# A transposed copy of the input for the first layer, and high and low weights side by side in a 136-column block

## The chip, the cores and the metric

The kernel runs on one core of a Trainium2 chip. The metric is the device time of one execution in microseconds (us). A core has five engines that run their own instruction streams in order: TensorE (PE: matmuls and transposes, results into PSUM), VectorE (DVE), ScalarE (ACT), GpSimd (POOL) and SyncE (SP). SyncE issues most of the DMAs here, ScalarE a few (`nc.scalar`).

## The reference, cut to what matters

Two layers of a gated mixer with 256 rows of 2048 channels. Each normalizes its input, multiplies it with a wide input matrix, runs four branches on slices of the product, and merges them by gates:

```python
def _layer(x, positions, norm_g, w_in, ..., w_up, merge_b, w_out):
    h = _rmsnorm(x, norm_g)
    proj = h @ w_in
    (a_q, a_k, a_v, a_z, b_cq, b_ckv, b_kr, b_z, c_qk, c_v, c_i, c_f, c_o, c_z,
     d_u, d_z, gate) = jnp.split(proj, idx, axis=-1)
    ya = _branch_dilated(a_q, a_k, a_v, a_qn_g, a_kn_g) * jax.nn.silu(a_z)
    yb = _branch_mla(...) * jax.nn.silu(b_z)
    yc = _branch_mlstm(...) * jax.nn.silu(c_z)
    yd = _branch_s5(...) * jax.nn.silu(d_z)
    up = jnp.einsum('bsnw,nwd->bsnd', jnp.stack([ya, yb, yc, yd], axis=2), w_up)
    gates = jax.nn.sigmoid((gate + merge_b).astype(jnp.float32)).reshape(Bsz, S, N_BRANCH, D_MODEL)
    merged = jnp.sum(gates * up.astype(jnp.float32), axis=2).astype(x.dtype)
    return x + merged @ w_out
```

`_rmsnorm` divides each row by the root of its mean square and scales it by `norm_g`. Branch d (`_branch_s5`) holds a linear recurrence along the rows.

## The kernel before

**Products in two parts.** Every weight tile `raw` (float32, by DMA) is split into a high part `wh` (a cast on ScalarE to the reduced format fp32r) and a low part `wl = raw − wh` (VectorE). The normalized input is split likewise into `hH` and `hL`. A product of one slice of 128 input channels (index k) and one half of the rows (t = 0, 1) is three matmuls into the same PSUM tile: `hH·wh`, `hH·wl`, `hL·wh`.

**Blocks and units.** A block is one slice of output columns over all k: 512 columns nearly everywhere, 136 in block `x`, which holds `b_ckv` (128 columns) and the gates `c_i`, `c_f` (8). The weights of a block come in units: 2 k of 512 columns, or 4 k of 136 (`_units`, L96). In layer 0 units 0 to 7 are block `cqkr`, 8 to 15 `du`, 16 to 19 `x`, 20 to 27 `cqk`; then come the other branch inputs (`aq1`, `ak1`, ... for branch a) with gate blocks (`g01`, ...) and their up-projections between them. A unit of 512 columns is 12 matmuls. `Stream` keeps three units split ahead and six loaded ahead; `raw`, `wh` and `wl` have four buffers each, so the load, the cast and the difference of a unit wait until the unit four before has been used.

**PSUM.** Large blocks take two of four banks `mm`, so the next block but one waits until the results have been read: by `aqk` (VectorE, blocks `aq` and `ak`), `gate` (VectorE, gate blocks), `bj`, `kr` and `blat` (ScalarE, blocks `cqkr` and `x`) and others.

**The order of the side work.** The program text is recorded once. All branch work is written as generators in chains; after each unit `tick` runs steps of them. `Plan` keeps an estimated clock for every engine and the estimated time at which every tile is ready, and `tick` takes a step when its inputs are ready by that estimate and no other engine's clock is too far ahead of TensorE's. The order of instructions on each engine thus follows from the estimates; on the chip the order is fixed and every engine follows it. Steps that matter below: `dm` (the scan of branch d along the rows), `dk` and `dr` (eight short steps that reduce an angle for branch d, VectorE), `rsi`, `rsy`, `rst`, `ass` (an inverse root by Newton steps, the first two on VectorE, the others on POOL), on which `aqk` depends.

**The start.** `win` unit 0 and the input come first on SyncE's queue (L1353 and following). The input tiles `xb` have the rows on the partitions; `prep_h` transposes them on TensorE (`xt`, 8 transposes of 128x128 for each of four chunks of 512 channels), and ScalarE and VectorE make `hH` and `hL` of the result. `squares` sums the squares of `xb` on ScalarE (`sq`, with a read of the accumulator after each); after the last one `finish_norm` reduces them (`r`, VectorE) and takes the inverse root on POOL. The norm factor `r` is applied when a block's result is read, so block `cqkr` can run before `r` is known, but `bj`, its first reader on ScalarE, waits for it. Eight matmuls on zeros (`warm`, L1352) stand at the very start.

All instructions of the engines are recorded through a helper, so the trace shows them with its line (L253 before), and all loads with L272.

Of the kernel before, what the change touches and what calls it, by code (L numbers as in the profile page):

```python
# [8 lines left out]
F32 = mybir.dt.float32  # L9
# [6 lines left out]
P = 128  # L16
S = 256
# [75 lines left out]
NCOL = {nm: len(c) for nm, c in COLS}  # L93


def _units(K, n):  # L96
    u = max(1, min(K, 1024 // n))
    while K % u:
        u -= 1
    return [(k0, u) for k0 in range(0, K, u)]  # L100
# [155 lines left out]


@with_exitstack
def hybrid_kernel(ctx: ExitStack, tc: tile.TileContext, x_in, pos, win, wup, wout, wuq, wukv, wglu, pp_in, db_in,
                  dc_in, glub_in, mb_in, cc_in, id_in, out, depth=2, dbg=None):  # L260
    nc = tc.nc
    plan = Plan(nc)
# [92 lines left out]
    class Stream:  # L355
# [5 lines left out]
        def dma(self, upto):  # L361
            while self.nd <= min(upto, len(units) - 1):
                _, dram, off, kk, n = units[self.nd]
                t = wp.tile([P, kk * n], F32, tag="raw", name="raw", bufs=4)
                load(nc.sync, t, in_=dram[off:off + P * kk * n].rearrange("(p f) -> p f", p=P))
                self.raw[self.nd] = t
                self.nd += 1

        def split(self, upto):
            while self.ns <= min(upto, len(units) - 1):  # L370
                self.dma(self.ns)
                i = self.ns
                _, _, _, kk, n = units[i]
                raw = self.raw.pop(i)
                wh = wp.tile([P, kk, n], F32R, tag="wh", name="wh", bufs=4)
                wl = wp.tile([P, kk, n], F32R, tag="wl", name="wl", bufs=4)
                rv = raw.rearrange("p (k n) -> p k n", n=n)
                if i >= 4:
                    for a, b in zip((wh, wl), self.names.pop(i - 4)):
                        plan.used[a.name] = plan.used[b]  # L380
                self.names[i] = (wh.name, wl.name)
                A.copy(wh, rv)
                V.tensor_tensor(wl, rv, wh, op=ALU.subtract)
                self.spl[i] = (wh, wl)
                self.ns += 1

        def get(self, i):
# [40 lines left out]
    def until(name, ready):  # L428
        while not ready() and step(name):
            pass  # L430

    def block(key, lhs, K, n):

        small = key[1] in ("uq", "ukv", "glu")
        ps = [brps(f"mb{t}") if small else mmps(f"mm{t}") for t in range(2)]
        if small:
            plan.pins.update(p.name for p in ps)
        k = 0
        while k < K:
            assert units[cur[0]][0] == key, (units[cur[0]][0], key)  # L440
            lhs(k, 0)
            wh, wl = stream.get(cur[0])
            if cur[0]:
                lhs(min(k + 4, K - 1), 0)
            kk = units[cur[0]][3]
            cur[0] += 1
            for j in range(kk):
                for t in range(2):
                    hH, hL = lhs(k, t)
                    o = ps[t][:, :n]  # L450
                    T.matmul(o, lhsT=hH, rhs=wh[:, j, :], start=(k == 0), stop=False)
                    T.matmul(o, lhsT=hH, rhs=wl[:, j, :], start=False, stop=False)
                    T.matmul(o, lhsT=hL, rhs=wh[:, j, :], start=False, stop=(k == K - 1))
                k += 1
            tick()
        if not small:
            drain("e")
        return ps
# [115 lines left out]
    def prep_h(o, d, xb):  # L574
# [17 lines left out]
                                       op0=ALU.mult, op1=ALU.subtract)  # L592
        o.hH[d], o.hL[d] = hH, hL

    def squares(o, d, xb):
        yield (xb,)
        for t in range(2):
# [15 lines left out]

    def lhs_of(H, Lo, chain="m"):
        def lhs(k, t):
            until(chain, lambda: Lo[k // 4] is not None)
            return H[k // 4][:, k % 4, t * P:(t + 1) * P], Lo[k // 4][:, k % 4, t * P:(t + 1) * P]

        return lhs
# [730 lines left out]
    ps = brps("warm")  # L1350
    for i in range(WARM):
        nc.tensor.matmul(ps, lhsT=zero[:, 0:P], rhs=zero, start=True, stop=True)  # L1352
    stream.dma(0)  # L1353
    for d in range(4):
        xb = s4([P, 2, 512], name="xb")
        if d == 0:
            for i in range(2):
                q = slice(256 * i, 256 * i + 256)
                load(nc.sync, xb[:, :, q], in_=x_cur[0][:, :, q])
        else:  # L1360
            load(nc.sync, xb, in_=x_cur[d])
        spawn("m", prep_h(o, d, xb))
        spawn("q", squares(o, d, xb))
        stream.dma(min(2 * d + 1, 3))
    load(nc.sync, cc, in_=cc_in)
    stream.split(0)
    step("m")
    spawn("q", rotary_tables())

    for l in range(depth):  # L1370
# [35 lines left out]
        for kind, nm in layer_sequence(l):  # L1406
            if kind == "in":
# [13 lines left out]
                    b_kr(o, ps)  # L1421
                    spawn("e", b_latent(o, ps, 448, 512, "cqg", "cqT"))
                elif nm == "x":
                    c_if(o, ps)
                    spawn("e", b_latent(o, ps, 128, 128, "ckvg", "ckT"))
                elif nm == "cqk":
                    o.cqk = copy_r(o, ps, 512, "cqk")
                    spawn("c", c_conv(o))
# [96 lines left out]
def _layout(inp):  # L1525
# [65 lines left out]
    for i, n in enumerate(("d_c_re", "d_c_im")):  # L1591
        a = f[n].reshape(dep, 16, 2, 16, 64).transpose(0, 2, 4, 1, 3)
        for g in range(2):
# [1 line left out]
    glu = f["d_glu_w"].reshape(dep, 2, 2, P, 512).transpose(0, 1, 3, 2, 4).reshape(dep, -1)  # L1595
    x = f["x"].reshape(2, P, D).transpose(1, 0, 2)
    pos = f["positions"].reshape(2, P).T
    arrs = dict(x_in=x, pos=pos, win=win, wup=wup, wout=wout, wuq=wuq, wukv=wukv, pp_in=pp,
                db_in=db.reshape(dep, P, 512), dc_in=dc.reshape(dep, P, 1024), wglu=glu, glub_in=f["d_glu_b"],
                mb_in=f["merge_b"], cc_in=_consts(), id_in=np.eye(P, dtype=np.float32))  # L1600
    return {k: np.ascontiguousarray(v) for k, v in arrs.items()}
# [18 lines left out]
```

## Time and profile before

| | us |
|---|---|
| median of 3 runs (lowest, highest) | 2090.07 (2087.39, 2090.59) |
| profiled execution | 2088.86 |
| its span in the trace | 2086.7 |
| TensorE busy | 2065.0 |
| VectorE busy | 1418.9 |
| ScalarE busy | 1034.8 |
| GpSimd busy | 446.9 |
| TensorE waiting for VectorE's `aqk`, `gate`, `wl` | 7.9, 3.9, 2.6 |

The span is that of one profiled execution on the chip. Busy time of TensorE counts matmuls whose ends are modelled, so it is an upper bound of its work; how long a matmul really occupies it is seen in the distance between the starts of two.

### The profile page before, as it was taken

The page shows a single profiled execution, that of the slowest core. Times are in us where ns is not written, and L with a number is a line of the kernel's source. Part 1 is how long each engine was busy: PE and PEld are TensorE (multiplying, and loading weights), DVE is VectorE, ACT ScalarE, POOL GpSimd, SP SyncE. Part 2 cuts the span into 40 slices and gives each one's busy share as a digit, 9 for nine tenths or more (in the row PEclk, how much of TensorE's full clock was granted, in tenths as well). Part 3 has the DMA queues.
Part 4 walks back from the last instruction along what each step waited for, and adds up shares of the span by engine and source line. Part 5 has one row for each costly group of instructions (what it writes and reads, how often), then busy time and mean ns, then how long its engine had stood idle before and what let it go on. Part 6 is the DMA issues. An engine that isn't in the chain of part 4 may idle for free.

```text
span 2086.7 us, 26821 instructions
## 1 busy us (share of the span) xinstructions
PE 2065.0 (99%) x9764; PEld 1702.1 (82%) x9764; DVE 1418.9 (68%) x1817; ACT 1034.8 (50%) x1574; POOL 446.9 (21%) x702
## 2 busy tenths in 40 slices
PE   9999999999999999999999999999999999999999
PEld 7888887788888888888888888887777888888887
DVE  5566578778777766667556765858777667667664
ACT  6656464454544544444456564455554445444442
POOL 2533114321242000001043121323223300001010
PEclk9999999999999999999999999999999999999999
DMA  7554354445555556656655543455445555556564
GB/s 266 182 187 166 123 176 167 156 163 170 183 191 173 183 199 206 204 202 208 232 188 182 192 162 124 175 166 191 163 167 187 185 178 183 205 204 205 197 212 171
DMA packets 111012, 384.60 MB, mean 184 GB/s; under 512 B 12321, under 2 KB 13217, under 8 KB 110881
## 3 DMA queue, kind: packets, MB, share of 16 engines
q1 hardware_dynamic: 108576, 378.40, 53.2%
q10 hardware_dynamic: 2304, 4.50, 0.6%
q8 instruction: 76, 1.25, 0.2%
q14 instruction: 56, 0.45, 0.1%
HBM read 378.66 MB, written 4.19 MB: 183 GB/s over the span
## 4 chain that ended last, share of the span: by engine, by line
PE 95%; DVE 3%; DMA 1%; POOL 1%; ACT 0%; issue 0%; SPq 0%; DVEq 0%; ACTq 0%
PE mm L253 86%; PE mb L253 2%; PE pv L253 1%; DVE dk L253 1%; PE tt L253 1%; PE dyp L253 1%; PE sc L253 1%; PE dbu L253 1%; DVE wl L253 1%; DVE dm L253 1%; DVE dr L253 1%; PE bsc L253 1%; PE pt L253 1%; DMA raw<-win 0%; PE xt L253 0%
## 5 line engine op out<-in xcount | busy, mean ns | idle before, releaser
L253 DVE TENSOR_TENSOR wl<-raw,wh 128x1024 fp32r<-128x1024 f32 (+1 forms) x694 | 909.0, 1323 | 533.8 <-ACT wh L253 530.8
L253 ACT CAST wh<-raw 128x1024 fp32r<-128x1024 f32 (+1 forms) x694 | 722.8, 1046 | 805.2 <-PE mm L253 690.7
L253 PE MATMUL mm<-wh,hH 128*128 128x512 f32 (+1 forms) x2240 | 877.0, 392 | 6.3 <-DVE gate L253 3.9
L253 PE MATMUL mm<-wl,hH 128*128 128x512 f32 (+1 forms) x2240 | 867.5, 387 | 2.6 <-DVE wl L253 2.6
L253 PE MATMUL mm<-wh,hL 128*128 128x512 f32 (+1 forms) x2240 | 866.7, 387 | 0.0
L253 PEld LDWEIGHTS mm<-wh,hH 128*128 128x128 f32 x2240 | 421.6, 188 | 97.5 <-issue 10.8
L253 PEld LDWEIGHTS mm<-wl,hH 128*128 128x128 f32 x2240 | 422.1, 188 | 88.0 <-DVE wl L253 5.5
L253 PEld LDWEIGHTS mm<-wh,hL 128*128 128x128 f32 x2240 | 421.6, 188 | 86.5 <-DVE hL L253 0.4
L253 POOL TENSOR_TENSOR gate<-gate 128x1024 f32<-128x1024 f32 x24 | 62.5, 2603 | 590.9 <-DVE gate L253 590.9
L253 POOL TENSOR_TENSOR dm<-dm,dm 128x256 f32<-128x256 f32 x64 | 76.3, 1213 | 354.9 <-DVE dm L253 345.9
L253 PE MATMUL mm<-wh,yH 128*128 128x512 f32 x256 | 101.3, 396 | 5.5 <-DVE aqk L253 5.5
L253 PE MATMUL mm<-wl,yH 128*128 128x512 f32 x256 | 100.6, 393 | 0.0
L253 PE MATMUL mm<-wh,yL 128*128 128x512 f32 x256 | 100.4, 392 | 0.0
L253 PE MATMUL mm<-wh,mH 128*128 128x512 f32 x256 | 100.2, 391 | 0.0
L253 PE MATMUL mm<-wh,mL 128*128 128x512 f32 x256 | 99.6, 389 | 0.0
L253 PE MATMUL mm<-wl,mH 128*128 128x512 f32 x256 | 99.6, 389 | 0.0
L253 POOL TENSOR_TENSOR dm<-dm,cosT 128x512 f32<-128x512 f32 x32 | 48.9, 1529 | 85.0 <-DVE dm L253 84.9
L253 PEld LDWEIGHTS mm<-wh,yH 128*128 128x128 f32 x256 | 48.7, 190 | 16.0 <-issue 5.9
L253 PEld LDWEIGHTS mm<-wh,yL 128*128 128x128 f32 x256 | 48.6, 190 | 10.2
L253 PEld LDWEIGHTS mm<-wl,yH 128*128 128x128 f32 x256 | 48.7, 190 | 9.8
L253 PEld LDWEIGHTS mm<-wh,mL 128*128 128x128 f32 x256 | 48.0, 188 | 9.9
L253 PEld LDWEIGHTS mm<-wh,mH 128*128 128x128 f32 x256 | 48.1, 188 | 9.8
(351 smaller groups left out, 1704.2 us busy)
## 6 DMA issues: line engine op xcount, KB each, us to landing
raw<-win SPq DMA_DIRECT2D x544, 512.0 KB, 3.7
raw<-wup SPq DMA_DIRECT2D x64, 512.0 KB, 4.2
raw<-wout SPq DMA_DIRECT2D x64, 512.0 KB, 4.2
mb<-mb_in SPq DMA_DIRECT2D x32, 256.0 KB, 4.4
xb<-x_in SPq DMA_DIRECT2D x7, 512.0 KB, 6.6
raw<-wuq SPq DMA_DIRECT2D x6, 512.0 KB, 4.1
raw<-win SPq DMA_DIRECT2D x8, 272.0 KB, 2.8
raw<-wglu SPq DMA_DIRECT2D x4, 512.0 KB, 4.4
```

What stands on the lines that cost most here:

```text
L253: return fn(*args, **kw)
```

## The change

The host lays out a second copy of the input, `xt_in`, with channels on the partitions (`x` reshaped and transposed). In layer 0, `prep_first` makes `hH` and `hL` from it, k by k, without TensorE and PSUM. The first load is chunk 0's slice k = 0, then unit 0 in two halves, then k = 1 to 3, all on SyncE; the other three chunks are issued by ScalarE. The untransposed `xb` are still needed for the squares: `first_squares` loads them on ScalarE's queue, the third and fourth each after the squares of an earlier one, and the constants `cc` after them. So the input is read twice.

In block `x`, a unit is 2 k instead of 4, `wh` and `wl` share one tile, and a (k, t) step is two matmuls: `hH` with `[wh | wl]`, 272 columns, and `hL` with `wh`, 136. The second half of the result is copied out of PSUM (`xlo`, ScalarE) and added to the first (VectorE); the readers of the block then take the sum from SBUF. This holds in both layers.

```diff
+NX = 136
 def _units(K, n):
-    u = max(1, min(K, 1024 // n))
+    u = max(1, min(K, 1024 // (2 * n if n == NX else n)))
...
-                load(nc.sync, t, in_=dram[off:off + P * kk * n].rearrange("(p f) -> p f", p=P))
+                src = dram[off:off + P * kk * n].rearrange("(p f) -> p f", p=P)
+                for q in (slice(0, n), slice(n, kk * n)) if self.nd == 0 else (slice(0, kk * n),):
+                    load(nc.sync, t[:, q], in_=src[:, q])
...
+                if n == NX:
+                    both = wp.tile([P, kk, 2, n], F32R, tag="wh", name="wh", bufs=4)
+                    wh, wl = both[:, :, 0], both[:, :, 1]
...
-                A.copy(wh, rv)
-                V.tensor_tensor(wl, rv, wh, op=ALU.subtract)
-                self.spl[i] = (wh, wl)
+                for q in (slice(0, 1), slice(1, kk)) if i == 0 else (slice(0, kk),):
+                    A.copy(wh[:, q], rv[:, q])
+                    V.tensor_tensor(wl[:, q], rv[:, q], wh[:, q], op=ALU.subtract)
+                self.spl[i] = (wh, both if n == NX else wl)
...
+                    if n == NX:
+                        two = [(ps[t][:, :2 * n], hH, wl[:, j].rearrange("p a n -> p (a n)")), (o, hL, wh[:, j])]
+                        for a, h, w in two if k < K - 1 else two[::-1]:
+                            T.matmul(a, lhsT=h, rhs=w, start=(k == 0 and h is hH), stop=(k == K - 1 and h is hH))
+                        continue
...
+    def prep_first(o, d, xt):
+        hH, hL = s4([P, 4, S], F32R, name="hH"), s4([P, 4, S], F32R, name="hL")
+        o.hH[d], o.hL[d] = hH, hL
+        for k2 in (0, 2):
+            yield (xt,)
+            for k in (k2, k2 + 1):
+                g = o.p("norm_g")[:, 4 * d + k:4 * d + k + 1]
+                A.activation(hH[:, k], xt[:, k], AF.Copy, scale=g)
+                V.scalar_tensor_tensor(hL[:, k], xt[:, k], g, hH[:, k].bitcast(F32), op0=ALU.mult, op1=ALU.subtract)
+            o.nh = 4 * d + k2 + 2
+
+    def first_squares(o):
+        xb = {}
+        yield
+        for d in range(5):
+            if d < 4:
+                xb[d] = s4([P, 2, 512], name="xb")
+                load(nc.scalar, xb[d], in_=x_cur[d])
+            else:
+                load(nc.sync, cc, in_=cc_in)
+            if d:
+                yield from squares(o, d - 1, xb[d - 1])
...
-    stream.dma(0)
+    first, o.nh = o, 0
     for d in range(4):
-        xb = s4([P, 2, 512], name="xb")
+        xt = s4([P, 4, S], name="xt")
         if d == 0:
-            for i in range(2):
-                q = slice(256 * i, 256 * i + 256)
-                load(nc.sync, xb[:, :, q], in_=x_cur[0][:, :, q])
+            load(nc.sync, xt[:, 0:1], in_=xt_in[:, 0:1])
+            stream.dma(0)
+            load(nc.sync, xt[:, 1:4], in_=xt_in[:, 1:4])
         else:
-            load(nc.sync, xb, in_=x_cur[d])
-        spawn("m", prep_h(o, d, xb))
-        spawn("q", squares(o, d, xb))
-        stream.dma(min(2 * d + 1, 3))
-    load(nc.sync, cc, in_=cc_in)
-    stream.split(0)
-    step("m")
+            load(nc.scalar, xt, in_=xt_in[:, 4 * d:4 * d + 4])
+        spawn("m", prep_first(o, d, xt))
+        if d == 0:
+            stream.dma(3)
+            step("m")
+            step("m")
+            stream.split(0)
+    spawn("q", first_squares(o))
...
-                    c_if(o, ps)
-                    spawn("e", b_latent(o, ps, 128, 128, "ckvg", "ckT"))
+                    lo = parp.tile([P, 2, NX], F32, tag="xlo", name="xlo", bufs=1)
+                    xs = [lo[:, t] for t in range(2)]
+                    for t in range(2):
+                        A.copy(xs[t], ps[t][:, NX:2 * NX])
+                    for t in range(2):
+                        V.tensor_tensor(xs[t], ps[t][:, :NX], xs[t], op=ALU.add)
+                    c_if(o, xs)
+                    spawn("e", b_latent(o, xs, 128, 128, "ckvg", "ckT"))
```

Since the estimates change, the planner also deals out layer 0's side work in another order. Three places follow. First ScalarE in block `cqkr` of layer 0, from the casts of units 5 to 7 to the first reader of the norm factor, before:

```order
L253 CAST wh<-raw 128x1024 x3
L253 ACTIVATE hH<-xt,pp 128x256 x4
L253 CAST wh<-raw 128x1024
L253 ACTIVATE sq,ss<-xb 128x512
L253 ACTIVATE dt<-pp 128x16
L253 CAST wh<-raw 128x1024
L253 ACTIVATE mag<-mag 128x16
L253 CAST wh<-raw 128x1024
L253 ACTIVATE bj,bss<-mm_132,r 128x64
```

and after, from the casts of units 6 to 8:

```order
L256 CAST wh<-raw 128x1024 x3
L256 ACTIVATE hH<-xt,pp 128x256 x2
L256 CAST wh<-raw 128x1024
L256 ACTIVATE sq,ss<-xb 128x512 x4
L256 ACTIVATE dt<-pp 128x16
L256 CAST wh<-raw 128x1024
L256 ACTIVATE mag<-mag 128x16
L256 ACTIVATE bj,bss<-mm_140,r 128x64
```

In both, ten units (1 to 10) and the first one have been cast when `bj` comes; four squares instead of one stand behind the cast of unit 9 (unit 8 before).

Second, VectorE in block `av1` of layer 0, around the reading of block `ak1` (`aqk`), before:

```order
L253 TENSOR_SCALAR rsi<-ass 128x8
L253 TENSOR_SCALAR rsy<-rsi 128x8
L253 TENSOR_TENSOR wl<-raw,wh 128x1024 x2
L253 SCALAR_TENSOR_TENSOR dm_3666<-mag,dm_3665 128x256 x2
L253 SCALAR_TENSOR_TENSOR dk<-cc,dhi,dk 128x256
L253 SCALAR_TENSOR_TENSOR dr<-cc,dlo,dk 128x256
...
L253 TENSOR_TENSOR wl<-raw,wh 128x1024
L253 TENSOR_TENSOR aqk<-mm_3496,ass 128x512
L253 TENSOR_TENSOR aqk<-mm_3497,ass 128x512
```

and after:

```order
L256 TENSOR_SCALAR rsi<-ass 128x8
L256 TENSOR_SCALAR rsy<-rsi 128x8
L256 TENSOR_TENSOR wl<-raw,wh 128x1024 x2
L256 TENSOR_TENSOR aqk<-mm_3441,ass 128x512
L256 TENSOR_TENSOR aqk<-mm_3442,ass 128x512
L256 TENSOR_TENSOR wl<-raw,wh 128x1024
L256 SCALAR_TENSOR_TENSOR dr<-cosT,dk 128x1024
```

The scan (`dm`, two steps) and the four pairs of `dk` and `dr` no longer stand between `rsy` and `aqk`; they now stand one block of branch a earlier, behind the reading of `aq1`, with two `gate` steps after them.

Third, TensorE in block `x`, one k, before:

```order
L253 MATMUL mm_642<-wh,hH 128x136
L253 MATMUL mm_642<-wl,hH 128x136
L253 MATMUL mm_642<-wh,hL 128x136
L253 MATMUL mm_643<-wh,hH 128x136
L253 MATMUL mm_643<-wl,hH 128x136
L253 MATMUL mm_643<-wh,hL 128x136
```

and two k after:

```order
L256 MATMUL mm_610<-wh,hH 128x272
L256 MATMUL mm_610<-wh,hL 128x136
L256 MATMUL mm_611<-wh,hH 128x272
L256 MATMUL mm_611<-wh,hL 128x136
L256 MATMUL mm_610<-wh,hH 128x272
L256 MATMUL mm_610<-wh,hL 128x136
```

Two matmuls take the place of three for each k and t.

## Rows read from the trace of the kernel before

**Rows 1.** Page, part 1: busy us of each engine, share, instructions

```profile
PE 2065.0 (99%) x9764; PEld 1702.1 (82%) x9764; DVE 1418.9 (68%) x1817; ACT 1034.8 (50%) x1574; POOL 446.9 (21%) x702
```

**Rows 2.** Waits of TensorE: us in total, times, longest

```profile
PE mm L253 <- DVE aqk L253: 7.9, 2, 5.5
PE mm L253 <- DVE gate L253: 3.9, 1, 3.9
PE mm L253 <- DVE wl L253: 2.6, 4, 1.6
```

**Rows 3.** Windows, layer 0: us; busy (count) PE, PEld, DVE, ACT, POOL; PEclk; DMA; GB/s

```profile
346.00:350.00 4.00, 2.68 (x12) 2.22 (x13) 4.00 (x5) 3.38 (x17) 0.54 (x1) 1.00 0.40 139
...
365.00:370.00 5.00, 5.00 (x17) 3.98 (x16) 2.73 (x3) 1.05 (x1) 1.55 (x2) 0.69 0.29 105
...
415.00:420.00 5.00, 2.25 (x5) 1.84 (x6) 4.96 (x8) 0.00 (x0) 0.00 (x0) 0.59 0.28 105
420.00:425.00 5.00, 5.00 (x18) 4.01 (x17) 1.48 (x2) 1.89 (x2) 0.00 (x0) 0.73 0.31 107
```

**Rows 4.** Timeline, TensorE, block `x`, layer 0 (96 of 136 columns): start, us, instruction

```profile
55.27 0.22 PE L253 MATMUL mm<-wh,hH 128*128 128x136 f32 x1
...
65.94 0.45 PE L253 MATMUL mm<-wh,hH 128*128 128x512 f32 x1
```

**Rows 5.** Chain that ended last: start, us, matmuls; `mb` has 256 columns, `mm` 512

```profile
118.20 2.87 PE mb L253 x24
121.08 9.09 PE mm L253 x40
```

**Rows 6.** Timelines, ScalarE and VectorE, and DMA landing: feeding one unit

```profile
58.10 1.05 ACT L253 CAST wh<-raw 128x1024 fp32r<-128x1024 f32 x1 [1.41 <-PE mm L253]
...
59.18 1.23 DVE L253 TENSOR_TENSOR wl<-raw,wh 128x1024 fp32r<-128x1024 f32 x1 [1.57 <-ACT wh L253]
...
raw<-win SPq DMA_DIRECT2D x8, 512.0 KB, 3.2
```

**Rows 7.** Timelines, VectorE and TensorE, at the two `aqk` waits

```profile
360.54 1.27 DVE L253 TENSOR_TENSOR_SCAN dm<-mag,dm 128x256 f32<-128x256 f32 x2
362.49 1.29 DVE L253 TENSOR_TENSOR aqk<-mm,ass 128x512 f32<-128x512 f32 x2 [0.68 <-POOL ass L253]
...
409.05 1.27 DVE L253 TENSOR_TENSOR_SCAN dm<-mag,dm 128x256 f32<-128x256 f32 x2
...
415.79 1.22 DVE L253 TENSOR_TENSOR wl<-raw,wh 128x1024 fp32r<-128x1024 f32 x1
416.93 1.28 DVE L253 TENSOR_TENSOR aqk<-mm,ass 128x512 f32<-128x512 f32 x2
...
417.75 0.77 PE L253 MATMUL mm<-wh,yH 128*128 128x512 f32 x1 [5.53 <-DVE aqk L253]
```

**Rows 8.** The start: chain, DMA landing at 8 to 12 us, window

```profile
8.32 3.52 PE mm L253 x12
11.85 0.87 PE xt L253 x8
12.72 2.77 PE mm L253 x12
...
raw<-win SPq DMA_DIRECT2D x2, 512.0 KB, 9.1
...
10.00:12.00 2.00, 2.00 (x12) 1.62 (x11) 1.33 (x2) 2.00 (x8) 0.00 (x0) 1.00 1.01 401
```

**Rows 9.** Timelines, ScalarE, VectorE and POOL: from the last square to `bj`

```profile
26.51 0.62 ACT L253 ACTIVATE sq<-xb 128x512 f32<-128x512 f32 x1
...
30.50 0.15 DVE L253 TENSOR_REDUCE r<-ss 128x2 f32<-128x8 f32 x1
...
37.52 0.20 POOL L253 TENSOR_TENSOR r<-rst,rsy 128x2 f32<-128x2 f32 x1
37.75 0.32 ACT L253 ACTIVATE bj<-mm,r 128x64 f32<-128x64 f32 x1 [5.71 <-POOL r L253]
```

More of the change, by code (lines that the diff above doesn't have):

```diff
@@ L258, in hybrid_kernel @@
 @with_exitstack
-def hybrid_kernel(ctx: ExitStack, tc: tile.TileContext, x_in, pos, win, wup, wout, wuq, wukv, wglu, pp_in, db_in,
+def hybrid_kernel(ctx: ExitStack, tc: tile.TileContext, x_in, xt_in, pos, win, wup, wout, wuq, wukv, wglu, pp_in, db_in,
                   dc_in, glub_in, mb_in, cc_in, id_in, out, depth=2, dbg=None):
@@ L374, in split @@
                 raw = self.raw.pop(i)
-                wh = wp.tile([P, kk, n], F32R, tag="wh", name="wh", bufs=4)
-                wl = wp.tile([P, kk, n], F32R, tag="wl", name="wl", bufs=4)
+                if n == NX:
+                    both = wp.tile([P, kk, 2, n], F32R, tag="wh", name="wh", bufs=4)
+                    wh, wl = both[:, :, 0], both[:, :, 1]
+                else:
+                    wh = wp.tile([P, kk, n], F32R, tag="wh", name="wh", bufs=4)
+                    wl = wp.tile([P, kk, n], F32R, tag="wl", name="wl", bufs=4)
                 rv = raw.rearrange("p (k n) -> p k n", n=n)
@@ L593, in prep_h @@
         o.hH[d], o.hL[d] = hH, hL
+    def prep_first(o, d, xt):
[15 more added lines that the diff above has]
+                load(nc.scalar, xb[d], in_=x_cur[d])
+            else:
+                load(nc.sync, cc, in_=cc_in)
+            if d:
+                yield from squares(o, d - 1, xb[d - 1])
     def squares(o, d, xb):
@@ L615, in lhs @@
         def lhs(k, t):
-            until(chain, lambda: Lo[k // 4] is not None)
+            until(chain, lambda: Lo[k // 4] is not None and (chain != "m" or Lo is not first.hL or first.nh > k))
             return H[k // 4][:, k % 4, t * P:(t + 1) * P], Lo[k // 4][:, k % 4, t * P:(t + 1) * P]
@@ L1597, in _layout @@
     pos = f["positions"].reshape(2, P).T
-    arrs = dict(x_in=x, pos=pos, win=win, wup=wup, wout=wout, wuq=wuq, wukv=wukv, pp_in=pp,
+    xt = f["x"].reshape(S, 16, P).transpose(2, 1, 0)
+    arrs = dict(x_in=x, xt_in=xt, pos=pos, win=win, wup=wup, wout=wout, wuq=wuq, wukv=wukv, pp_in=pp,
                 db_in=db.reshape(dep, P, 512), dc_in=dc.reshape(dep, P, 1024), wglu=glu, glub_in=f["d_glu_b"],
```

## The prediction

> **What bounds the kernel now.** I read the busy shares first: TensorE works 99% of the span, VectorE 68%, ScalarE 50% [rows 1]. So a saving counts only where TensorE issues less, waits less or runs at a higher granted clock. The waits of TensorE come next: two waits for `aqk` hold 7.9 us, one for `gate` 3.9, four for `wl` 2.6 [rows 2]. Then the stretches around the waits of layer 0: at 346 us TensorE is busy only 2.68 of 4 us, and after the two `aqk` waits the granted clock is 0.69, 0.59 and 0.73 in the five-microsecond windows, between the 1.2 and the 2.4 GHz level [rows 3]. The price of a matmul comes from the x block and from the chain [rows 4, 5], the price of feeding one from ScalarE and VectorE [rows 6], the two `aqk` waits from the timelines [rows 7], and the start from the chain, a DMA row and the rows that lead to `r` [rows 8, 9]. The profiled execution took 2088.86 us, 1.2 under the median 2090.07; I sum against the former and add 1.2 at the end. 4.2 us (0.2%) is about what a measurement of this kernel can tell from no change.
>
> **The x block.** Its 96 matmuls of 136 columns run from 55.27 to 65.94 us, 10.67 us, 111 ns each [rows 4]. A 512-column matmul is 9.09/40 = 227 ns, a 256-column one 2.87/24 = 119.6 ns [rows 5]. So 136 columns sit on a floor that does not shrink with the columns. A matmul of 272 columns appears nowhere; on the line through 256 and 512 columns it is 119.6 + 16 × 107.4/256 = 126 ns. Its bounds are 119.6 (no dearer than 256) and 227. The middle of these is no better guess than the line, since 272 lies next to 256, so I take 126. A (k, t) step then costs 126 + 111 = 237 instead of 333 ns: 96 ns less, 32 steps a layer, two layers: −6.1 us. The added work is small: two copies, two adds and eight more weight-tile DMAs, on engines that have room; the x block's result is read a block later and nobody on TensorE waits for it soon. What shrinks is the cover. The block gets shorter, 7.6 instead of 10.7 us, and is cut into units of two k. The first unit of the next block needs a raw buffer that the fifth x unit gives back at about block start + 2.1; its load lands 3.2 later, cast 1.05 and difference 1.23 follow [rows 6], which is start + 7.6 with the gaps between them, where TensorE wants it at + 7.6. I charge 0.7 us for both layers (0 to 2.6, the upper end if each layer waits for a whole 1.23 us difference). **Net −5.4** (−6.1 to −3.5).
>
> The Trainium skill, page "TensorE: Matmul & The Clock Gate", section "Back-to-back issue gap", gives an isolated gap of N/2.4 + 2.5 ns, that is 59 ns for 136 and 116 for 272 columns; by that the fusion would save 2.5 ns a pair, 0.2 us in all. The row of 111 ns [rows 4] speaks against it here; a saving near zero is a rival below all the same.
>
> **The order of layer 0.** The edits change the planner's clocks, so layer 0's side work is dealt out anew, layer 1's not. Two waits lie there. The first: block `aq1`'s evacuation `aqk` starts at 362.49, behind a scan and a POOL result, while TensorE stands [rows 7]. The second: a scan starts at 409.05, eight `dk`/`dr` steps follow, `wl` at 415.79, and `aqk` only at 416.93; TensorE resumes at 417.75 after 5.53 us [rows 7]. In the changed order both `aqk` pairs come ahead of the scan and the eight steps: the first has its POOL chain started two units (5.4 us) earlier and comes one `wl` earlier, the second has no burst ahead of it. Cost now: `wl` 1.6 us near 347 [rows 2, 3]; 7.9 us of `aqk`; and the clock: 17 matmuls where 22 fit in 365 to 370 us (−1.1), 5 × 227 ns of work in 2.25 busy us (−1.1) and 18 for 22 (−0.9) after the second [rows 3]. Sum 1.6 + 7.9 + 3.1 = 12.6. What is late next: the burst now stands after the first `aqk` with two `gate` steps behind it. By the rows it occupies 415.79 − 409.05 = 6.7 us, and two `gate` steps about as long as two `aqk`, 1.3 [rows 7], then `wl` 1.23: 9.3 us from one `wl` to the next. Usually these lie 2.72 us apart (twelve matmuls at 227 ns) and each is done 8.2 − 2.3 = 5.9 us before TensorE needs it, since its buffer comes free three units ahead [rows 6]. 9.3 − 2.7 − 5.9 = 0.7 us of wait. A later `aqk` (block `aq2`) stands two units lower than before, behind the `wl` that is done 2.3 us after the last unit ahead of the block that wants its banks has begun; that unit lasts 2.7, the two steps 1.3, so 0.3 to 0.9 of wait: 0.7. **Gain 12.6 − 1.4, −11** (−12.6 to −5, the latter if one wait of the second's size, 5.5 + 2.0, comes back). The `gate` wait of 3.9 us is in layer 1 and stays [rows 2].
>
> **The start, first twelve units.** Three groups of eight transposes leave TensorE, 0.87 us each [rows 8]: −2.6. The first matmul needs 1 MB landed, as before, but no transposes between: I put it at 7.6 instead of 8.3, −0.7. The first twelve matmuls cost 3.52 us against 2.77 later, with the transposes just ahead of them [rows 8]; with nothing ahead of them since the warm-up I double that loss: +0.8 (0 to 1.5). ScalarE now multiplies every chunk from `xt`, and its squares wait for `xb`, which is loaded on ScalarE's own queue behind three `xt` chunks. In order behind those squares stand the casts of units 2, 5 and 6. Loads ran at 401 GB/s here and a weight tile took 9.1 us to land [rows 8], so 2 MB more in the same stretch is 5 us of transfers. I charge 2.4 us of waits (0 to 4). These four terms cancel: unit 11 would start at about 41.7 us, as before.
>
> The Trainium skill, "DMA: Bandwidth & Descriptors", section "Issuing engines are not separate DMA queues", says that loads started by different engines interleave on the same 16 DMA engines; by it the charge tends to its upper end, 1.6 us more. No run here shows two large streams from two queues.
>
> **The start, the norm.** ScalarE's `bj` waits for `r`: the last square at 26.51 us, the reduction at 30.50, `r` done at 37.72, `bj` at 37.75 after 5.71 us idle [rows 9]. Behind `bj` stands the cast of unit 11. Before, one more square was left at that point; now four are, and all behind the cast of unit 9, whose buffer TensorE frees at 41.7 − 5 × 2.72 = 28.1. Cast 1.05: 29.2; four squares with their accumulator reads, 0.8 each: 32.4; cast of unit 10 and two small steps: 33.7; its `wl`, 34.9, stands ahead of the reduction; then the same 7.2 us: `r` at 42.2. `bj` and `kr` 1.0, cast 1.05, `wl` 1.23: 45.5. TensorE wants it at 41.9: a wait of 3.6 us, and at the clock's price of the waits above (1.1 after 2.3 us, 2.0 after 5.5) another 1.4. **Start +5** (0 to +8).
>
> **Sum.** 2088.86 − 5.4 − 11 + 5 = 2077.5; with 1.2 for the median: **2078.5 us**.
>
> **The rivals.** *No wait for the norm.* The wait before left 5.71 us of idle on ScalarE without stopping TensorE; if the last `xb` lands early and the casts run ahead, the start costs nothing: 2090.07 − 5.4 − 11 = 2073.7. Against it: four squares in a row behind a late cast. 0.18. *One wait comes back in layer 0*, at the burst with the two gates, of the second's size: 2090.07 − 5.4 − 5 + 5 = 2084.7, and with the upper start 2087.7: about half of this is within no change. 0.22. *The other side:* the burst of scan and eight steps stands at three places of layer 0; if TensorE waited at each as at 412 us (5.5 + 2.0), the order would give +22.5 − 12.6 = +10 and the time is 2090.07 − 5.4 + 10 + 5 = 2099.7, slower. It decides from the third wait on. Against it: at the other two places no evacuation stands directly behind the burst. 0.05. *The fusion saves nothing*: 272 columns take what two of 136 take, 222 ns, near the 227 of 512 columns [rows 4, 5]; then the block is not shorter either, and the time is 2090.07 − 11 + 5 = 2084.1. Against it the 119.6 ns of 256 columns. 0.03. By the rule of the Trainium skill named above it would be 2083.9.
>
> **How the numbers follow.** The forecast case, 2075 to 2083, gets the remaining 0.52. The bounds of the terms reach from 2071 (all low) to 2089.6 (all high); leaving out the ends, I give 2070 to 2087. Faster by over 0.2% (below 2085.9): 0.52 + 0.18 + 0.03 and 0.09 of the wait that comes back = 0.82; within: 0.13; slower: 0.05.
>
> **What would show it.** In the changed profile: the x block's steps 237 ns apart, 64 matmuls in 7.6 us a layer; no `xt` transposes; TensorE's `aqk` waits gone, a `wl` wait below 1.5 us after the burst; a `wh` or `wl` wait of 3 to 4 us at unit 11 near 42 us, with ScalarE's `bj` waiting for `r`; the gate wait of 3.9 unchanged. The prediction is wrong if the x block takes over 9 us, if an `aqk`, `gate` or `wl` wait over 3 us shows in layer 0 outside the start, or if the start loses over 8 us.

## The result and the profile after

The changed kernel takes 2077.16 us (median of 4 runs, 2075.86 to 2079.51) against 2089.86 of the kernel before (4 runs, 2087.39 to 2090.59): ratio 0.9943, 95% interval 0.9925 to 0.996. That is faster, by 12.7 us, where 11.6 were forecast (2078.5 against 2090.07). The profiled execution, the fastest of the four, took 2075.86 us with a span of 2074.0, 12.7 less than before; all stretches below are read from it alone.

The page's first part and the waits of TensorE after the change (waits: us in total, times, longest) answer to [rows 1, 2]:

```profile
PE 2054.5 (99%) x9668; PEld 1691.5 (82%) x9668; DVE 1417.6 (68%) x1830; ACT 1037.7 (50%) x1587; POOL 438.7 (21%) x702
```

```profile
PE mm L256 <- ACT wh L256: 6.7, 2, 4.2
PE mm L256 <- DVE gate L256: 3.9, 1, 3.9
PE mm L256 <- DVE wl L256: 2.8, 6, 0.8
...
PE mm L256 <- DVE aqk L256: 0.4, 1, 0.4
```

The two long `aqk` waits are gone, one of 0.4 us is left; the `gate` wait of layer 1 is what it was. New is `wh` from ScalarE: 4.2 us of it is the wait for the first weights (the kernel before waited for `xb` there), the rest, 2.6 us, is at unit 11.

Where the time went can be read at three marks, the starts of block `x`'s first matmul in either layer and of the second matmul behind the block. Before, they stand at 55.27 [rows 4] and 66.23 us in layer 0 and at 1096.64 and 1107.60 in layer 1 (TensorE's timeline: start, us, instruction):

```profile
66.23 0.40 PE L253 MATMUL mm<-wl,hH 128*128 128x512 f32 x1
...
1096.64 0.22 PE L253 MATMUL mm<-wh,hH 128*128 128x136 f32 x1
...
1107.60 0.40 PE L253 MATMUL mm<-wl,hH 128*128 128x512 f32 x1
```

After, it shows in layer 0

```profile
60.40 0.38 PE L256 MATMUL mm<-wh,hH 128*128 128x272 f32 x1
...
62.86 0.34 PE L256 MATMUL mm<-wh,hH 128*128 128x272 f32 x1
63.03 0.23 PE L256 MATMUL mm<-wh,hL 128*128 128x136 f32 x1
63.09 0.34 PE L256 MATMUL mm<-wh,hH 128*128 128x272 f32 x1
...
69.14 0.50 PE L256 MATMUL mm<-wl,hH 128*128 128x512 f32 x1 [0.40 <-DVE wl L256]
```

and in layer 1

```profile
1086.70 0.28 PE L256 MATMUL mm<-wh,hH 128*128 128x272 f32 x1
...
1094.62 0.50 PE L256 MATMUL mm<-wl,hH 128*128 128x512 f32 x1
```

| stretch | before | after | difference | forecast |
|---|---|---|---|---|
| start to block `x`, layer 0 | 55.27 | 60.40 | +5.1 | +5 |
| block `x`, layer 0 | 10.96 | 8.74 | −2.2 | |
| block `x`, layer 1 | 10.96 | 7.92 | −3.0 | −5.4 for both |
| between the two blocks | 1030.41 | 1017.56 | −12.9 | −11 |
| behind block `x` of layer 1 | 979.1 | 979.4 | +0.3 | 0 |

In the block, a 272-column and a 136-column matmul follow each other in 63.09 − 62.86 = 0.23 to 0.24 us, as forecast (237 ns).

The start: TensorE at its first weights, at the rise of the clock and at unit 11, and the windows (us; busy and count of PE, PEld, DVE, ACT, POOL; PEclk; DMA share; GB/s) with the clock beside them:

```profile
8.68 0.79 PE L256 MATMUL mm<-wh,hH 128*128 128x512 f32 x1 [4.15 <-ACT wh L256]
...
14.26 0.43 PE L256 MATMUL mm<-wh,hH 128*128 128x512 f32 x1
...
44.25 0.50 PE L256 MATMUL mm<-wh,hH 128*128 128x512 f32 x1 [2.58 <-ACT wh L256]
45.51 0.79 PE L256 MATMUL mm<-wl,hH 128*128 128x512 f32 x1 [0.76 <-DVE wl L256]
```

```profile
8.00:14.00 6.00, 5.33 (x12) 3.92 (x13) 4.57 (x8) 4.27 (x9) 0.00 (x0) 0.50 1.02 417
46.00:48.00 2.00, 2.00 (x6) 1.52 (x6) 2.00 (x3) 2.00 (x5) 0.00 (x0) 0.50 0.75 252
```

The first twelve matmuls take 14.26 − 8.68 = 5.58 us at a granted clock of 0.50, the 1.2 GHz level, where [rows 8] had 3.52 and a granted clock of 1.00 from 10 to 12 us. Unit 11 waits 2.58 us for its high part and 0.76 for its low part, and again the granted clock is 0.50 behind the wait. The rows that lead to it answer to [rows 9]; ScalarE (casts of units 8 and 9, the last square), VectorE, POOL and ScalarE again:

```profile
27.29 1.05 ACT L256 CAST wh<-raw 128x1024 fp32r<-128x1024 f32 x1 [1.06 <-DMA raw<-win]
...
30.07 1.05 ACT L256 CAST wh<-raw 128x1024 fp32r<-128x1024 f32 x1 [0.93 <-DVE hL L256]
...
32.88 0.62 ACT L256 ACTIVATE sq<-xb 128x512 f32<-128x512 f32 x1
...
35.81 0.15 DVE L256 TENSOR_REDUCE r<-ss 128x2 f32<-128x8 f32 x1
...
36.49 0.17 DVE L256 TENSOR_SCALAR rsy<-rsi 128x2 int32<-128x2 int32 x1
...
38.70 0.22 POOL L256 TENSOR_TENSOR trf<-trf,trt 128x16 f32<-128x16 f32 x1
38.88 0.19 POOL L256 TENSOR_TENSOR rst<-rsy 128x2 f32<-128x2 f32 x1
...
41.92 0.20 POOL L256 TENSOR_TENSOR r<-rst,rsy 128x2 f32<-128x2 f32 x1
...
42.16 0.31 ACT L256 ACTIVATE bj<-mm,r 128x64 f32<-128x64 f32 x1 [7.41 <-POOL r L256]
...
43.14 3.89 ACT L256 CAST wh<-raw 128x1024 fp32r<-128x1024 f32 x4
```

The last square stands at 32.88, `r` is there at 42.1, and ScalarE has been idle for 7.41 us when `bj` starts; the cast of unit 11 is the first of the four at 43.14. VectorE's two steps of the root end at 36.66, but POOL starts its twelve only at 38.88: nine steps of branch d's angle (`tr`, `trt`, `trf`), the last of them at 38.70, stand ahead of them in its order.

Layer 0's order: VectorE at its burst, answering to [rows 7], the one wait that TensorE has there, and the window around it:

```profile
358.43 1.28 DVE L256 TENSOR_TENSOR aqk<-mm,ass 128x512 f32<-128x512 f32 x2
...
361.15 1.27 DVE L256 TENSOR_TENSOR_SCAN dm<-mag,dm 128x256 f32<-128x256 f32 x2
...
367.93 1.41 DVE L256 SCALAR_TENSOR_TENSOR gate<-mm,r,mb 128x512 f32<-128x512 f32 x2
369.25 4.62 DVE L256 TENSOR_TENSOR wl<-raw,wh 128x1024 fp32r<-128x1024 f32 x4
```

```profile
370.52 0.50 PE L256 MATMUL mm<-wl,hH 128*128 128x512 f32 x1 [0.53 <-DVE wl L256]
```

```profile
366.00:371.00 5.00, 4.47 (x20) 3.42 (x19) 4.93 (x9) 2.26 (x3) 0.00 (x0) 1.00 0.00 0
```

`aqk` follows without idle time, its POOL result being there; the burst with its two `gate` steps occupies 361.15 to 369.25; the wait that it makes is 0.53 us, and in the window around it, the last row, the granted clock stays at 1.00 where [rows 3] had 0.69 and 0.59 behind the waits.

### The profile page after: what moved, and what is told of

Its sections match the earlier page's. It is cut to its first block, busy times and chain, and to the rows that moved or that the text cites. A ratio compares the mean times of both kernels' runs of the same rounds, so it can differ in the third digit from the quotient of the medians.

```text
span 2074.0 us, 26684 instructions
## 1 busy us (share of the span) xinstructions
PE 2054.5 (99%) x9668; PEld 1691.5 (82%) x9668; DVE 1417.6 (68%) x1830; ACT 1037.7 (50%) x1587; POOL 438.7 (21%) x702
## 4 chain that ended last, share of the span: by engine, by line
PE 93%; DVE 3%; DMA 1%; ACT 1%; POOL 1%; issue 1%; SPq 0%; DVEq 0%; ACTq 0%
PE mm L256 84%; PE mb L256 2%; PE pv L256 1%; DVE wl L256 1%; PE tt L256 1%; DMA raw<-win 1%; PE dyp L256 1%; PE sc L256 1%; PE dbu L256 1%; ACT wh L256 1%; DVE dk L256 1%; PE pt L256 1%; DMA xt<-xt_in 1%; PE bsc L256 1%; DVE dr L256 0%
## 5 line engine op out<-in xcount | busy, mean ns | idle before, releaser
L256 ACT CAST wh<-raw 128x1024 fp32r<-128x1024 f32 (+2 forms) x703 | 723.9, 1035 | 794.1 <-PE mm L256 685.3
L256 PE MATMUL mm<-wl,hH 128*128 128x512 f32 x2176 | 851.3, 391 | 2.9 <-DVE wl L256 2.8
L256 PEld LDWEIGHTS mm<-wl,hH 128*128 128x128 f32 x2176 | 410.0, 188 | 89.7 <-DVE wl L256 7.3
L256 POOL TENSOR_TENSOR dm<-dm,dm 128x256 f32<-128x256 f32 x64 | 71.4, 1137 | 360.7 <-DVE dm L256 359.7
L256 POOL TENSOR_TENSOR dn<-dm,dr 128x512 f32<-128x512 f32 x32 | 56.5, 1767 | 0.0
```

What stands on the lines that cost most here:

```text
L256: return fn(*args, **kw)
```

## The experiments

The questions: which part of the change brings what, whether layer 0's gain belongs to the change at all or to the order that the planner happens to give, and what holds the start. Each kernel was timed in three rounds against the kernel before, whose medians in these sessions were 2088.8 to 2089.4. The changed kernel itself was not timed in them; its four runs lie 3.7 us apart, so a difference of 2 or 3 us to it rests on the traces as much as on the medians.

**The fused block alone.** The kernel before with the diff's parts on `NX`, `both`, `two` and `xlo`, and with the old start:

```diff
-    u = max(1, min(K, 1024 // n))
+    u = max(1, min(K, 1024 // (2 * n if n == NX else n)))
...
+                        two = [(ps[t][:, :2 * n], hH, wl[:, j].rearrange("p a n -> p (a n)")), (o, hL, wh[:, j])]
```

> The kernel before with the fused 136-column block alone; the start is the old one with the transposes. The planner deals out layer 0 in the changed kernel's order (burst behind the first aqk, gates after it). Theory (the new order comes from any shift of the planner's clocks, the start only costs): block x saves 5.3 us over both layers, layer 0 loses 2.0 instead of 14.2 us around its waits, the start stays (block x begins at 55.3 us): 2089.9 - 5.3 - 12.2 = 2072.4 us, ratio 0.992, faster than the changed kernel. Rival (the transposed start brings the new layer-0 gain): only the block's 5.3 us, 2084.6 us.

Measured: 2074.41 us (2073.27 to 2075.16), ratio 0.9931 (0.9917 to 0.9946). Block `x` of layer 0 begins at 55.82 us and the two long `aqk` waits are gone, although the transposes are still there. Behind the block two waits appear that the other kernels don't have, of TensorE for a `wl` and for the gates' POOL chain (waits with the idle time in brackets):

```profile
96.07 0.50 PE L256 MATMUL mm<-wl,hH 128*128 128x512 f32 x1 [0.60 <-DVE wl L256]
...
111.51 0.38 PE L256 MATMUL cg<-ident,gi 128*4 128x128 f32 x2 [1.54 <-POOL gi L256]
```

These 2.1 us are about what it is short of the expected 2072.4. So this one part alone gives layer 0's new order and is at least as fast as the whole change (2.8 us less by the medians, though the two intervals overlap). Block `x` takes 7.95 and 7.91 us here, 6.1 us less than before in the two layers.

**The transposed start alone.** The changed kernel with block `x` put back:

```diff
-    u = max(1, min(K, 1024 // (2 * n if n == NX else n)))
+    u = max(1, min(K, 1024 // n))
...
-                        two = [(ps[t][:, :2 * n], hH, wl[:, j].rearrange("p a n -> p (a n)")), (o, hL, wh[:, j])]
```

> The changed kernel with block x as before (units of 4 k, three matmuls a step). Layer 0's order around aqk is again the changed kernel's. Theory: the start costs 5.1 us (block x begins at 60.4 us, a wait of 3.3 us for unit 11), the order gains 12.2: 2089.9 + 5.1 - 12.2 = 2082.8 us. Rival (the start pays for itself, since 32 transposes are gone): block x begins before 55.3 us and the time is below 2077.5.

Measured: 2082.91 us (2081.61 to 2084.03), ratio 0.9971 (0.996 to 0.9982), as the theory said to 0.1 us, but this is luck: block `x` begins at 62.02 us, after waits of 2.51 and 0.67 us at unit 11, so the start cost 6.8 us in this trace, not 5.1, and the stretch between the two blocks gained 13.2, not 12.2. The start costs time; the kernel is still faster than before, through the order.

**The order alone.**

```diff
+                if l == 0 and nm == "cqk":
+                    plan.clk["DVE"] += 2000.0
                 ps = proj(nm)
```

> The kernel before with one line more: the planner's estimate of VectorE's clock is raised by 2 us ahead of block cqk of layer 0. No work is added or removed; layer 0's evacuations stand in the changed kernel's order. Theory: the waits at 347, 361 and 412 us and the low clock after them go, 12 us: 2077.8 us, with a remaining wl wait of about 0.5. Rival (the shorter block x or the shorter PSUM use made the waits go): they stay, 2090 us, or turn up at another evacuation.

Measured: 2078.02 us (2074.94 to 2079.59), ratio 0.9952 (0.9935 to 0.9968). Nothing of the computation or the loads is changed by this line. The waits of TensorE:

```profile
PE mm L253 <- DVE gate L253: 3.9, 1, 3.9
PE mm L253 <- DVE wl L253: 2.3, 6, 0.5
...
PE mm L253 <- DVE aqk L253: 0.4, 1, 0.4
```

No `aqk` wait above 0.4 is left, no `wl` wait above 0.5. One number in the planner gives 11 us, nearly as much as the whole change.

**The change in the old order.**

```diff
+                if l == 0 and nm == "ak0":
+                    plan.clk["PE"] += 1500.0
                 ps = proj(nm)
```

> The changed kernel with one line more: the planner's estimate of TensorE's clock is raised by 1.5 us ahead of block ak0 of layer 0. All of the change is in, but around aqk layer 0's side work stands as in the kernel before. Theory (layer 0's gain is the order alone): the waits of 1.6, 2.3 and 5.5 us and the low clock behind two of them come back, 12 us: 2077.2 + 12.2 = 2089.4 us, no faster than the kernel before. Rival (the change has made room, so that the old order no longer waits): 2077 us.

Measured: 2089.96 us (2089.38 to 2091.56), ratio 1.0004 (0.9994 to 1.0013): the change is worth nothing in the old order. TensorE waits where the kernel before waited:

```profile
350.58 0.50 PE L256 MATMUL mm<-wl,hH 128*128 128x512 f32 x1 [1.62 <-DVE wl L256]
367.20 0.47 PE L256 MATMUL mm<-wh,hH 128*128 128x512 f32 x1 [2.91 <-DVE aqk L256]
421.57 0.77 PE L256 MATMUL mm<-wh,yH 128*128 128x512 f32 x1 [5.53 <-DVE aqk L256]
```

The last one is the same 5.53 us to the last digit. The two runs together show it from both sides: layer 0's gain comes from the order, and the two intended parts cancel (−5.5 in the block and +6.1 in the start here, −5.3 and +5.1 in the changed kernel). All traces agree: between the two blocks `x` the two kernels in the old order take 1030.4 and 1030.7 us, the ten in the new order, the fused block alone left aside, 1016.9 to 1018.0.

**`bj` later.** In the changed kernel, the four readers of `r` on ScalarE are kept back while the planner counts them as before:

```diff
+                    A._hold = [] if l == 0 else None
                     b_kr(o, ps)
-                    spawn("e", b_latent(o, ps, 448, 512, "cqg", "cqT"))
+                    held, A._hold = A._hold or [], None
+
+                    def late(held=held, o=o, ps=ps):
+                        for f, a, kw in held:
+                            f(*a, **kw)
+                        yield from b_latent(o, ps, 448, 512, "cqg", "cqT")
+
+                    spawn("e", late())
```

> The changed kernel with the four readers bj and kr of layer 0 issued four casts later on ScalarE (behind the cast of unit 14, directly ahead of blat); every other engine's order is unchanged. Theory (the cast of unit 11 waits behind bj for r): the wait of 3.3 us at unit 11 and the 1.3 us at the low clock behind it go, block x begins at 55.7 us: 2077.2 - 4.7 = 2072.5 us. Rival (the cast of unit 11 is held by something else as well, a load or its buffer): a wait of the same length stays at unit 11 to 15, 2077 us.

Measured: 2076.68 us (2076.18 to 2076.95), ratio 0.9942 (0.9928 to 0.9957), no gain. The cast of unit 11 starts at 34.84, so `bj` had indeed held it, and the wait at unit 11 is gone; but another comes at the start of block `x`, which wants block `cqkr`'s banks, and block `x` then runs at a granted clock of 0.50 from 60 to 64 us and takes 10.9 us instead of 8.0 up to the next block. `blat` reads these banks last, after a second inverse root (`bss`) that POOL makes behind the first. TensorE's row, and POOL's for the last steps to `r`:

```profile
58.56 0.50 PE L259 MATMUL mm<-wh,hH 128*128 128x272 f32 x1 [2.96 <-ACT blat L259]
```

```profile
42.27 1.21 POOL L259 TENSOR_TENSOR rst<-rst,r 128x2 f32<-128x2 f32 x1
43.56 1.13 POOL L259 TENSOR_SCALAR rst<-rst 128x2 f32<-128x2 f32 x1
44.78 0.20 POOL L259 TENSOR_TENSOR rsy<-rst,rsy 128x2 f32<-128x2 f32 x1
```

`r` is ready at 46.1 here instead of 42.1, because four of POOL's steps take 1.1 to 1.2 us instead of 0.2. So the edit delayed `r` itself, and the run can't tell what a later `bj` alone would bring; it shows that here the chain on POOL to `r` and on to `bss` holds the start in another place.

**The roots on VectorE.** The Newton steps of the roots of layer 0's norm and of its `b_latent` move to VectorE, 9 steps each instead of 12; every other order stays. `b_latent` runs twice, so three roots move, not two; the third, of block `x`, stands at 74 us, behind the start:

```diff
+            if dve:
+                nc.vector.tensor_tensor(t, y, y, op=ALU.mult)
+                nc.vector.scalar_tensor_tensor(t, t, -0.5, z, op0=ALU.mult, op1=ALU.mult)
+                nc.vector.scalar_tensor_tensor(z if i == 2 else y, t, 1.5, y, op0=ALU.add, op1=ALU.mult)
...
-        rsqrt(r)
+        rsqrt(r, dve=o is first)
...
-        rsqrt(ss)
-        G.tensor_tensor(ss, ss, o.r, op=ALU.mult)
+        rsqrt(ss, dve=o is first)
...
```

> The changed kernel with the Newton steps of two inverse roots of layer 0 (that of the norm, r, and that of block cqkr's b_cq part, bss) on VectorE instead of POOL, 9 short steps each; all other orders are unchanged, bj stands where it stood. Theory (what bounds the start is the chain of POOL steps that makes r and then frees block cqkr's banks): r is ready at 38.5 instead of 42.2 us, the wait of 3.3 us at unit 11 shrinks below 0.5, the second wait seen with the later bj does not appear, block x begins near 56 us: 2077.2 - 4.5 = 2072.7 us. Rival (loads hold the casts, as the input is read twice): the wait stays at unit 11 or just behind it, 2076.5 us.

Measured: 2071.01 us (2070.48 to 2073.14), ratio 0.9914 (0.9899 to 0.9928), 6 us under the changed kernel by the medians; the two traces differ by 2.7 (spans 2071.3 and 2074.0), since this kernel's profiled execution was its slowest and the other's its fastest. VectorE's last step, ScalarE's `bj` and TensorE's first matmul of block `x`:

```profile
38.69 0.16 DVE L496 SCALAR_TENSOR_TENSOR r<-rst,rsy 128x2 f32<-128x2 f32 x1
...
38.95 0.31 ACT L256 ACTIVATE bj<-mm,r 128x64 f32<-128x64 f32 x1 [3.76 <-DVE posf L256]
...
55.84 0.28 PE L256 MATMUL mm<-wh,hH 128*128 128x272 f32 x1
```

`r` comes 3.3 us earlier, no wait is left at unit 11, and block `x` begins 4.6 us earlier, 0.6 later than before the change. The kernels with this start bear it out together: block `x` begins at 55.8 to 57.8 us in the four with the roots on VectorE, and at 60.4 to 63.6 in the four with `r` on POOL in which neither `bj` nor the loads were touched. With the chain out of the way, the transposed copy neither gains nor loses against the transposes up to block `x`; the old start with the roots on VectorE was not run. Behind block `x` TensorE now waits 0.46 and 0.76 us for a unit whose load landed late, so 3.9 of the 4.6 us are left there.

The edit does two things at once. From the end of `rsy` to `r` the changed kernel takes 5.5 us, this one 1.8. Of the 3.7 between them, 2.2 are the nine angle steps that stood ahead of the root in POOL's order, and only 1.5 are the steps themselves (3.24 for twelve on POOL, 1.73 for nine on VectorE). Leaving the root on POOL and putting the angle steps behind it was not tried; 2.2 of 3.7 us would be more than half of the gain (an estimate from these rows).

**The input read once.** The changed kernel with the squares taken of the transposed tiles (their sums are not the norm's) and the second reading left out (`Quiet` issues nothing), in the same order:

```diff
-                load(nc.scalar, xb[d], in_=x_cur[d])
+                load(Quiet(), xb[d], in_=x_cur[d])
...
+                src = o.xt[d].rearrange("p (a k) s -> p a (k s)", a=2)
+                nc.scalar.activation(sq, src[:, t], AF.Square, accum_out=o.ss[:, t, d:d + 1])
```

> The changed kernel without the second reading of the input in layer 0: the squares are taken of the transposed tiles, so the sums of squares are not the norm's; order and number of all other instructions are unchanged, 2 MB less are loaded. Theory (the wait at unit 11 is mostly the POOL chain to r and the order on ScalarE): the cast of unit 9 starts at 27.9 instead of 30.1 us, r is ready some 1.5 us earlier, the wait of 3.3 us shrinks to about 1.8: 2075.4 us. Rival (the second reading is what makes the start slow): the whole loss of the start, 4.5 us, goes: 2072.5 us.

Measured: 2073.23 us (2073.11 to 2074.46), ratio 0.9923 (0.9909 to 0.9938), between the two. `r` is done at 40.5 (40.7 followed from the theory), unit 11 waits 0.64 and 0.75 us, block `x` begins at 57.90, 2.5 us earlier, and 3.4 and 4.1 earlier than in the kernel in the old order and in the one with the transposed start alone. By block `x`'s start the 2 MB cost half of the start's loss, by the medians (3.9 us) more; the theory had them too small. The cast of unit 9 starts at 28.40, behind a buffer of TensorE, where it stood at 30.07 behind a late load.

**A longer warm-up.**

```diff
-S4B, H2B, WARM = 33, 9, 8
+S4B, H2B, WARM = 33, 9, 26
```

> The changed kernel with 26 instead of 8 matmuls on zeros at the very start, so that TensorE works until the first weights are there. Theory: the first twelve matmuls run at the higher clock and units 1 to 10 come 2.8 us earlier, but unit 11 still waits for r, whose chain hangs on loads and ScalarE: its wait grows from 3.3 to about 6 us and the time stays at 2077. Rival (the chain to r follows TensorE by the buffers it frees): the whole 2.8 us come through, 2074.4 us.

Measured: 2078.55 us (2077.7 to 2079.82), ratio 0.995 (0.9933 to 0.9966). This doesn't settle the theory against the rival. The 384 KB of `xt` landed 2 us later than in the changed kernel, TensorE was idle again between the warm-up and the first weights, and the first twelve matmuls still took 4.8 us, at a granted clock of 1.00 up to 12 us and of 0.55 behind it (ScalarE's wait for `xt`, TensorE's first matmul):

```profile
9.58 0.51 ACT L256 ACTIVATE hH<-xt,pp 128x256 fp32r<-128x256 f32 x1 [4.03 <-DMA xt<-xt_in]
...
10.65 0.51 PE L256 MATMUL mm<-wh,hH 128*128 128x512 f32 x1 [1.53 <-ACT wh L256]
```

**Both.** The roots on VectorE and 26 matmuls on zeros.

> Both edits, the roots on VectorE and 26 matmuls on zeros. Theory: r at 38.5 us with unit 11 wanted at about 38.7 instead of 41.5: a wait of about 3 us comes back, nearly all of the gain of the warmer start is lost again, 2072.5 us. Rival: both gains add, 2070 us.

Measured: 2071.68 us (2071.22 to 2072.68), ratio 0.9916 (0.9901 to 0.993), the same as with the roots alone. The load landed late here too (ScalarE starts on it at 9.26 us), so this is no test of the sum either.

**Layer 1 in another order.** Since the `gate` wait of layer 1 also stands behind a burst of scan and eight steps, the kernel with the roots on VectorE was given two other orders of layer 1:

```diff
+                if l == 1 and nm == "ak0":
+                    plan.clk["PE"] += 2500.0
```

> The kernel with the roots on VectorE and the planner's estimate of TensorE's clock raised by 2.5 us ahead of block ak0 of layer 1 only, which deals out layer 1's side work anew: the burst of scan and dk/dr steps no longer stands ahead of the gate of block az. Theory (a burst ahead of an evacuation makes the wait, in layer 1 as in layer 0): the gate wait of 3.9 us goes and with it about 1 us of low clock, 2072.7 - 5 = 2067.7 us. Rival: the burst costs as much at its new place, 2072.7 us.

Measured: 2069.44 us (2068.76 to 2070.06), ratio 0.9904 (0.9889 to 0.9919). The `gate` wait is gone and an `aqk` wait of 4.01 us stands at 1387.61 us in its place: mostly the rival. The second:

```diff
+                if l == 1 and nm == "g21":
+                    plan.clk["PE"] += 4000.0
```

> The roots on VectorE, and the planner's estimate of TensorE's clock raised by 4 us ahead of block g21 of layer 1, another order of layer 1: the burst of scan and dk/dr steps no longer stands ahead of the gate of block az, while the evacuations before it keep their places. Theory: the gate wait of 3.9 us goes and none over 1 us takes its place: 2071.0 - 4.5 = 2066.5 us. Rival: another evacuation waits as long, as aqk of block ak0 did for 4.0 us in the other new order of layer 1: 2069 to 2071 us.

Measured: 2067.75 us (2067.1 to 2068.18), ratio 0.9895 (0.9879 to 0.9912), the fastest of all. The `gate` wait is gone and the longest in its stretch is one for a `wl`:

```profile
1492.72 0.50 PE L256 MATMUL mm<-wl,yH 128*128 128x512 f32 x1 [1.41 <-DVE wl L256]
```

3.3 us less than with the roots alone by the medians, where 4.5 were expected. In the traces the stretch behind block `x` of layer 1, where the order changed, takes 975.1 us against 980.3 with the roots alone and 979.4 in the changed kernel, so 4.3 to 5.2 less, `wl` wait included; the start took 2.0 us back in this execution (block `x` of layer 0 at 57.81 instead of 55.84). This kernel beats the changed one by 9.4 us by the medians.

## Why the prediction was right

**The total** was right to 1.3 us, and its three terms nearly so: −5.3 for −5.4 (block `x`), −12.9 for −11 (layer 0's order, a little beyond the bound of −12.6), +5.1 for +5 (start). The terms add up to 2078.7, not to the 2078.5 that was written. The runs with one part each confirm the signs, and that the prediction had split them rightly: the order was told apart from the edits' own work. Their sizes move with the execution: the start cost 5.1, 6.1 and 6.8 us in three kernels with the same start, and block `x` alone saved 6.1 us.

**Block `x`.** The line through 256 and 512 columns gave the 237 ns that were measured. By the isolated gap that the Trainium skill, page "TensorE: Matmul & The Clock Gate", section "Back-to-back issue gap", gives, the fusion would have saved next to nothing. The section itself calls that gap too small for a stream of narrow matmuls. Here two matmuls of 136 columns took 222 ns by [rows 4], and one of 272, with the 136 beside it at 111 as before, 237 − 111 = 126, so the measurement decides against the isolated gap. The charge for the shorter cover, 0.7 us, seems to have been 0.8, but only half of this is the cover: the block has 7.6 us of work a layer, and with the first matmul behind it (0.3 us) would take 7.9; layer 1 took 7.92, layer 0 8.74, of it 0.40 a wait for `wl`. Another 0.28 is TensorE's third matmul in the block, which starts at 60.91, right after `blat` has read the bank it wants (60.86): this belongs to the chain to `r` and `bss`.

**Layer 0's order.** The mechanism and the places were right: the two `aqk` waits went, the burst at its new place made a wait of 0.53 us (forecast 0.7), the later `aqk` one of 0.39 (forecast 0.7). Mis-sized was the cost before. I took 1.6 + 7.9 + 3.1 = 12.6 us; summed over the starts of matmuls around the three waits, what lies over 227 ns a matmul is 1.9 + 4.2 + 5.7 + 2.4 = 14.2 us before, and 2.0 at the three waits after. Of the difference of 1.6, 1.1 is low clock outside the windows that I counted in; 0.5 is in the three waits, whose own figures start at the modelled end of the matmul before.

**The start.** The sum was right by luck in its first part. The first matmul came at 8.68, not 7.6 (before, the timeline has it at 8.04; the 8.32 of [rows 8] is where the chain enters); the first twelve cost 5.58 us, where 4.3 had been forecast (3.52 of [rows 8] and 0.8); the 2.4 us of waits for ScalarE did not come at all. Unit 11 was wanted at 41.5 us, forecast 41.7: three misses that cancel. The chain to `r` had the right steps in the right order and the right end: `r` at 42.1 (forecast 42.2), `wl` of unit 11 at 45.5 (45.5), the wait 3.3 us (3.6). In between two misses cancel, which is luck too. The cast of unit 9 started 2.0 us late, at 30.07 instead of 28.1, and not for the cause given: it was held not by TensorE's buffer but by late loads. The cast of unit 8 waited for its load, and that of unit 9 came 0.1 us after its own had landed at 29.97; its row names `hL`, which ended at the same moment, but in the eight other kernels with both readings the row names the load. The run with one reading shows the loads to cost about 2.5 us of the start. These 2 us were won back behind it: the four squares took 2.5 us instead of 3.2, and the stretch from the reduction to `bj` 6.3 instead of the same 7.2, mainly because one angle step on POOL that had taken 1.12 us before now took 0.22.

**The rivals.** No order with a burst waited 5.5 us in the changed kernel, so neither the reversal nor the slower case arose. That they were possible the old order shows: with it the change is no faster.

## What to carry to other kernels

Where a planner's estimates set the order, any edit deals the work out anew, and the new order can be worth more than the edit: time the edit's parts apart, and time the order alone (one line that shifts an estimate) and the edit in the old order. A wait for a small result is best followed through all its readers before one of them is moved, and through all that stands ahead of its makers; here the chain of short steps was the thing to shorten, and more than half of it was other work ahead of it on POOL. A matmul so narrow that fewer columns make it no cheaper is worth widening.

## What the runs showed of the hardware

A POOL step on 128x2 or 128x16 numbers takes 0.2 us while VectorE is idle, and 1.1 to 1.2 us while a `wl` runs on VectorE, about that one's length (1.23): in the run with the later `bj` four such steps moved `r` by 4 us, where the root's steps of [rows 9] ran beside an idle VectorE. In the changed kernel all 124 such steps that ran beside an idle VectorE took 0.3 us or less, and 25 of the 26 that began well inside a `wl` over 0.9. It works the other way round as well: the `dk` and `dr` steps of the burst on VectorE take 0.46 to 0.49 us, but 1.4 to 1.5 while a POOL step on 128x512 runs (VectorE, then POOL, changed kernel):

```profile
362.83 1.40 DVE L256 SCALAR_TENSOR_TENSOR dr<-cc,dlo,dk 128x256 f32<-128x256 f32 x1
364.15 1.51 DVE L256 SCALAR_TENSOR_TENSOR dk<-cc,dhi,dk 128x256 f32<-128x256 f32 x1
...
362.50 1.44 POOL L256 TENSOR_TENSOR dm<-dm,cosT 128x512 f32<-128x512 f32 x1 [3.58 <-DVE dm L256]
363.90 1.48 POOL L256 TENSOR_TENSOR dn<-dm,dr 128x512 f32<-128x512 f32 x1
```

Two of the eight are stretched so in the kernel before as well, at 412.06 and 413.59, just ahead of the `aqk` that TensorE waits 5.53 us for: about 2 us of the burst's 6.7 are this. The Trainium skill, page "SBUF — State Buffer", section "🔬 SBUF: two separate sides", says that VectorE with two inputs from SBUF and GpSimd hold a shared pair of ports one at a time; the rows agree with it in both directions.

The landing of the 384 KB of `xt` at the very start varies more than expected: 5.5 to 6.9 us after its issue in eight kernels with the same first loads, 7.1 and 7.4 in the two with 26 matmuls on zeros. Whether the longer warm-up has to do with it is open. It moves TensorE's first matmul (8.68 to 10.65 us) and the kernel with it: block `x` begins 3.2 us later with the longer warm-up alone, and 2.0 later in the last run above than with the roots alone (first matmul at 10.11 and 8.96), so marks of the start from one execution are good to about 2 us only.
